# Half a weight tile of large products issued as one block, and the state's products placed later in the chain

## The chip, the core and the metric

The kernel runs on one core of a Trainium2 chip. Each engine of the core works through its own queue in order: TensorE (PE, matrix products), VectorE (DVE), ScalarE (ACT), GpSimd (POOL) and SyncE (SP, which issues DMAs). The metric is the device time of one execution in microseconds; for the kernel before, the median of three runs.

## The reference, cut to what matters

Two layers run over 256 context tokens and 512 latent tokens of width 1024. In each, one input projection feeds three branches; their results are projected, gated, summed and projected again, and an MLP of four times the width follows.

```python
zc, zl = hc @ w_in, hl @ w_in                 # context, latent
def _rwkv_scan(state0, r, decay, k, v, kk, a, reverse):
    def step(S, inp):                         # per head of 64
        s_kk = einsum('bhij,bhj->bhi', S, kk_t)
        S = S * w_t - s_kk * (kk_t * a_t) + v_t * k_t
        return S, einsum('bhij,bhj->bhi', S, r_t)
# branch A: this scan, forward and backward, 16 heads, context before latent
# branch B: depthwise convolution of 31 taps, LayerNorm, silu
# branch C: attention, 8 query heads of 128, 2 key heads
out = sum(gates * (branch @ w_branch)) @ w_out
x = x + rms_norm(out); x = x + rms_norm(square(relu(h @ w1)) @ w2)
```

Layer 1, the last, needs only the latent tokens of the output.

## The kernel before

**Large products.** Every product with a weight matrix is split into three 32-bit products (high by high, low by high, high by low: `hh`/`hl` of the activations, `wh`/`wl` of the weights). A weight column of 128 outputs has eight k-tiles of 128. Half of it (four k-tiles, 128x512) is one transfer: SP issues the DMA into `raw`, ACT makes `wh` from it (L328), POOL or DVE makes `wl` (L330, L332). `fill` (from L397) takes k-tiles from a list of jobs and issues their products on L412. So half a weight tile gives four k-tiles times three terms times the pieces of the tokens: 24 products in layer 0 (768 tokens, two pieces of 384), 12 in most of layer 1 (512 tokens, one piece). The MLP uses `gemm` (L389) instead.

**The rwkv phase.** Branch A walks over eight pairs of heads in each layer. Tokens are cut into 12 chunks of 64. For one pair, in this order: merge of the inverse's blocks (L892, L904), a batch of products (L920, L931), and the chain of 12 steps. A step adds to the state's accumulator `sp` a product that no state enters (L952) and one that the state enters (L956); ACT scales it into the new state `S` (L958); the outputs `yp` take a product of the state (L968) and one without it (L970). Beside the chain run the readout of the pair before (L1005, L1016) and the preparation of the next one: squares of the keys (L717, L700 for their sums by head), the low-rank products (L1032), the scaled keys on DVE (L772 to L784), the bonus (key on L871, product on L877, used on L878). Then come the grams of the next pair (L810, masked on DVE by L814; transposes on L819), and then the solve: DVE inverts triangular blocks by 30 alternating small operations (L861, L862) between transposes (L855, L856 and L863, L864), while PE has the rest of the pair's preparation (L743, L845). The next merge needs L863 and L864. In between DVE evicts what large products deliver: operands of branch A (L658, `in_k`, `in_r`, `in_v`), branch B's input (L463), and it does the 31 taps of the convolution (L473), which are held in program order.

**What sets the order.** The program states a weave: `weave` takes generators, each of which yields an estimate of its time on PE, and calls `fill` in proportion, so that large products are strewn between the small ones. Tile's scheduler then orders each engine's queue by dependence and priority; a product may move past others whose operands are not expected yet. `fill` is also called in attention between the score products (L615) and the transposes of the probabilities (L631) of a block of queries. At the end of each pair `fill` is called for a fixed number of k-tiles that lie over the solve.

Of the kernel before, what the change touches and what calls it, by code (L numbers as in the profile page):

```python
# [8 lines left out]
F32 = mybir.dt.float32  # L9
# [67 lines left out]
class Kern:  # L77
# [314 lines left out]
    def job(s, src, mh, ml, T, done, pre=None):  # L392

        s.halves += [(src, h) for h in range(2)]
        s.jobs += [(k, mh, ml, T, done, pre) for k in range(KT)]

    def fill(s, n=1):  # L397
        nc = s.nc
        for _ in range(min(n, len(s.jobs))):
            k, mh, ml, T, done, pre = s.jobs.pop(0)  # L400
            if k % 4 == 0:
                while s.halves and len(s.ready) < 2:
                    s.ready.append(s.weight_half(*s.halves.pop(0)))
                s.cur = s.ready.pop(0)
            if k == 0:
                s.jps = s.mm()
                s.jctx = (pre(),) if pre else ()
            wh, wl = s.cur
            for w, m, f in ((wh, mh, 0), (wh, ml, 1), (wl, mh, 2)):
                a = m(k)  # L410
                for b, t0, t1 in s.pieces(T):
                    ins = nc.tensor.matmul(s.jps[:, b, :t1 - t0], lhsT=w[:, k % 4, :], rhs=a[:, t0:t1], start=k == 0 and f == 0, stop=k == KT - 1 and f == 2)  # L412
                    if s.pin and f == 0 and b == 0:
                        s.tc.keep_in_program_order(ins)
            if k == KT - 1:
                done(s.jps, *s.jctx)
# [292 lines left out]
    def rw_kk(s, P, p, I):  # L709

        nc = s.nc
        kkc = P['v']('rw_k_k')[:, p:p + 1]
        sq = s.rt("ksq", [128, TOK], alias="a1")
        nc.scalar.activation(out=sq, in_=I['k'], func=AF.Square, scale=kkc)
        sp = s.g([128, 6, 2])
        for t in range(6):
            nc.tensor.matmul(sp[:, t, :], lhsT=sq[:, t * 128:t * 128 + 128], rhs=s.bo[:, 0:128:64], start=True, stop=True)  # L717
# [20 lines left out]
    def rw_transpose(s, src, h, dst):  # L738

        nc = s.nc  # L740
        vp = s.g([128, 6, 64])
        for m in range(6):
            nc.tensor.transpose(out=vp[:, m, :], in_=src[ROWS[h], m * 128:m * 128 + 128], identity=s.ident[ROWS[h], 64 * h:64 * h + 64])  # L743
        nc.scalar.activation(out=dst(0), in_=vp[ROWS[0]], func=AF.Copy)
        nc.scalar.activation(out=dst(1), in_=vp[ROWS[1]], func=AF.Copy)
# [43 lines left out]
    def rw_front(s, I, Q, d, g, lat):  # L789
# [18 lines left out]
        for q in range(4):  # L808
            for h in range(2):
                nc.tensor.matmul(gp[h][:, q, 0:n, :], lhsT=BK[ROWS[h], 4 * g + q].rearrange("p a b -> p (a b)"),  # L810
                                 rhs=KR[ROWS[h], 0:n, 4 * g + q, :], start=True, stop=True)
# [6 lines left out]
        for q in range(4):  # L818
            nc.tensor.transpose(out=bk[:, q].rearrange("p a b -> p (a b)"), in_=BK[:, 4 * g + q].rearrange("p a b -> p (a b)"), identity=s.ident)  # L819
        nc.scalar.activation(out=GB[:, :, c, 0, :], in_=bk.rearrange("p c h j -> p h c j"), func=AF.Copy)  # L820
# [15 lines left out]
    def rw_rest(s, d):  # L836
# [3 lines left out]
        for g, m in ((0, 8), (8, 4)):  # L840
            mv = s.g([128, 8, 64])
            for c in range(g, g + m):
                for h in range(2):
                    w = ROWS[1 - h]
                    nc.tensor.matmul(mv[ROWS[h], c - g, :], lhsT=GL[w, h, c, :], rhs=UV[w, h * 12 + c, :], start=True, stop=True)  # L845
            nc.scalar.activation(out=KM[:, g:g + m, 1, :], in_=mv[:, :m], func=AF.Copy)
            yield 0.16 * m
# [18 lines left out]
    def rw_bonus(s, P, p, I, Q, T):  # L866
# [8 lines left out]
        for b, t0, t1 in s.pieces(T):  # L875
            bp = s.g([128, t1 - t0])
            nc.tensor.matmul(bp, lhsT=s.bo, rhs=ks[:, t0:t1], start=True, stop=True)  # L877
            nc.vector.tensor_tensor(out=bv[:, t0:t1], in0=I['v'][:, t0:t1], in1=bp, op=ALU.mult)  # L878
            yield 0.8
# [3 lines left out]
    def rw_merge(s, Q, d):  # L883
# [6 lines left out]
        for q in range(12):  # L890
            for h in range(2):
                nc.tensor.matmul(xp[two[h], q, :], lhsT=GL[one[h], h, q, c:c + 32], rhs=Dn[one[h], q, :], start=True, stop=True)  # L892
        TT = Q['TT', d] = GL.rearrange("p h c t -> p (h c t)")[:, 0:768].rearrange("p (c t) -> p c t", t=64)
# [8 lines left out]
        for q in range(12):  # L902
            for h in range(2):
                nc.tensor.matmul(tr[one[h], q, :], lhsT=Xn[two[h], q, :], rhs=Dt[two[h], q, :], start=True, stop=True)  # L904
        for h in range(2):
# [3 lines left out]
    def rw_batch(s, Q, d, lat):  # L909
# [6 lines left out]
        for q0 in range(0, 12, 4):  # L916
            wu = s.g([128, 4, 2, 64])
            for q in range(q0, q0 + 4):
                for h in range(2):
                    nc.tensor.matmul(wu[ROWS[h], q - q0], lhsT=TT[ROWS[h], q, :], rhs=KM[ROWS[h], q].rearrange("p a b -> p (a b)"), start=True, stop=True)  # L920
            nc.scalar.activation(out=W[:, q0:q0 + 4], in_=wu[:, :, 0, :], func=AF.Copy)
# [4 lines left out]
        for q0 in range(0, 12, 4):  # L926
            n = 1 if lat and q0 == 0 else 2
            ap = s.g([128, 4, 2, 64])
            for q in range(q0, q0 + 4):
                for h in range(2):  # L930
                    nc.tensor.matmul(ap[ROWS[h], q - q0, 0:n, :], lhsT=W[ROWS[h], q, :], rhs=GB[ROWS[h], h, q, 0:n, :], start=True, stop=True)  # L931
            nc.vector.tensor_tensor(out=KR[:, 0, q0:q0 + 4, :], in0=ap[:, :, 0, :], in1=s.id2.unsqueeze(1).to_broadcast([128, 4, 64]), op=ALU.add)
# [4 lines left out]
    def rw_chain(s, Q, lat, note, free):  # L937
# [5 lines left out]
        for k in range(NCH):  # L943
            q = (k, ORD_B[k])
            need_y = not lat or k >= 4
            seg = 0 if k < 4 else 1
            if k < NCH - 1:
                sp = s.pc.tile([128, 2, 64], F32, tag="c", name="sp")
                Sn = t("S", [128, 2, 64], 2)
                for d in range(2):  # L950
                    for h in range(2):
                        nc.tensor.matmul(sp[ROWS[h], d], lhsT=GB[d][:, h, q[d], 0, :], rhs=UV[d][:, h * 12 + q[d], :], start=d == 0, stop=d == 1 and k == 0)  # L952
                if k:
                    for d in range(2):
                        for h in range(2):
                            nc.tensor.matmul(sp[ROWS[h], d], lhsT=KR[d][ROWS[h], 0, q[d], :], rhs=S[ROWS[h], d], start=False, stop=d == 1)  # L956
                for d in range(2):
                    nc.scalar.activation(out=Sn[:, d], in_=sp[:, d], func=AF.Copy, scale=Q['lam', d][:, q[d]:q[d] + 1])  # L958
            if need_y:
                fresh = seg not in yp  # L960
                if fresh:
                    yp[seg] = s.py.tile([128, 512], F32, tag="y", name="yp")
                for part in ((1, 0) if k else (0,)):
                    for d in range(2):
                        o = (q[d] - 4 * seg) * 64
                        for h in range(2):
# [15 lines left out]
    def rw_readout(s, l, P, p, Q, T, dst):  # L982
# [19 lines left out]
        for b, t0, t1 in s.pieces(T):  # L1002
            R = s.g([128, t1 - t0])
            for c in range(t0, t1, 128):
                nc.tensor.transpose(out=R[:, c - t0:c - t0 + 128], in_=y[:, c:c + 128], identity=s.ident)  # L1005

# [7 lines left out]
        for b, t0, t1 in s.pieces(T):  # L1014
            gp = s.g([128, t1 - t0])
            nc.tensor.matmul(gp, lhsT=Q['g2'], rhs=s.sgd[:, t0:t1], start=True, stop=True)  # L1016
            nc.vector.tensor_tensor(out=y[:, t0:t1], in0=y[:, t0:t1], in1=gp, op=ALU.mult)
# [109 lines left out]
    def rwkv_phase(s, l, P, T):  # L1127
# [3 lines left out]
        with ExitStack() as rc:  # L1131
# [315 lines left out]
```

## Time and profile before

| | |
|---|---|
| median of three runs | 4514.72 us (4509.4 to 4517.8) |
| the profiled execution | 4503.07 us |
| its span, first to last instruction | 4501.3 us |
| mean granted clock of TensorE, as a share of full speed | 0.956 |
| busy PE, DVE, ACT, POOL | 93%, 59%, 42%, 18% |
| large products: L412, L389 (instructions) | 8520, 4608 |

The profile shows one execution. In its rows an instruction is named by its engine, line and operation, then the tile written and the tiles read. A small 32-bit product can leave two records, so that x8 in a row can be four products. Starts are in microseconds from the start of the span; the start of one product to the start of the next says how long it held PE, since the printed duration includes the pipeline. A window gives the busy time of the engines in a stretch. "128*128" behind an operation is the rows and columns of the array that it uses.

### The profile page before, as it was taken

To read this page: it belongs to the slowest core of one execution; us is meant where nothing else is said; L and a number is where in the kernel's file an instruction comes from. 1 tells how busy PE (TensorE), PEld (TensorE's weight loads), DVE (VectorE), ACT (ScalarE), POOL (GpSimd) and SP (SyncE) were. 2 spreads that over 40 slices of the span, in tenths; PEclk is the share of its full clock that TensorE was granted. 3 is DMA by queue.
4 is the path that set the end of the run, shared out by engine and by line. 5 is a ranking of instruction groups with operands and counts; after the bars stand their busy time and mean duration, and the time that the engine had idled before them with its cause. 6 is when DMAs were issued, how large, how long until landed. Compare 5 with 4: busy or idle time off the path is not lost. (4 is left out here: it accounts for less than half of the span.)

```text
span 4501.3 us, 76922 instructions
## 1 busy us (share of the span) xinstructions
PE 4197.0 (93%) x31232; PEld 3411.4 (76%) x31232; DVE 2642.9 (59%) x4762; ACT 1889.5 (42%) x3690; POOL 831.3 (18%) x737
## 2 busy tenths in 40 slices
PE   6999999999998989899999899999999988898998
PEld 4888888888786668689999667877777775475886
DVE  3788788887855443132233568778787845443344
ACT  3455445444534442232223354555555534434333
POOL 0011221212112144300000102122122212262001
PEclk8999999999999999999999889999999979998998
DMA  4211111111224234343322221111111223142332
GB/s 161 62 47 53 57 58 57 51 52 58 73 84 157 71 110 142 126 141 117 107 87 63 69 61 52 50 60 47 56 54 57 75 71 121 57 133 64 96 96 82
DMA packets 438346, 364.05 MB, mean 81 GB/s; under 512 B 19022, under 2 KB 386792, under 8 KB 431848
## 3 DMA queue, kind: packets, MB, share of 16 engines
q1 hardware_dynamic: 417256, 279.43, 20.5%
q10 hardware_dynamic: 20736, 79.70, 4.9%
q8 instruction: 247, 4.05, 0.4%
q14 instruction: 107, 0.88, 0.1%
HBM read 299.29 MB, written 53.48 MB: 78 GB/s over the span
## 5 line engine op out<-in xcount | busy, mean ns | idle before, releaser
L328 ACT ACTIVATE wh<-raw 128x512 fp32r<-128x512 f32 x700 | 441.4, 631 | 1261.5 <-PE mm L389 558.3
L330 POOL TENSOR_TENSOR wl<-raw,wh 128x512 fp32r<-128x512 f32 x388 | 535.5, 1381 | 2062.3 <-ACT wh L328 1699.1
L412 PE MATMUL mm<-hh,wh 128*128 128x384 f32 (+1 forms) x2072 | 668.6, 381 | 49.4 <-ACT wh L328 40.7
L412 PE MATMUL mm<-hl,wh 128*128 128x384 f32 (+1 forms) x2072 | 644.5, 370 | 7.0 <-POOL hl L330 7.0
L412 PE MATMUL mm<-hh,wl 128*128 128x384 f32 (+1 forms) x2072 | 641.4, 369 | 4.9 <-POOL wl L330 4.6
L332 DVE TENSOR_TENSOR wl<-raw,wh 128x512 fp32r<-128x512 f32 x312 | 215.5, 691 | 589.7 <-ACT wh L328 586.4
L412 PEld LDWEIGHTS mm<-hh,wh 128*128 128x128 f32 x2072 | 379.2, 195 | 112.7 <-ACT wh L328 45.6
L473 DVE SCALAR_TENSOR_TENSOR cv<-u,dw,cv 128x783 f32<-128x783 f32 (+1 forms) x480 | 458.3, 955 | 3.1
L412 PEld LDWEIGHTS mm<-hl,wh 128*128 128x128 f32 x2072 | 389.6, 195 | 47.7 <-issue 12.1
L412 PEld LDWEIGHTS mm<-hh,wl 128*128 128x128 f32 x2072 | 388.0, 194 | 47.1 <-POOL wl L330 10.8
L412 PE MATMUL mm<-oh,wh 128*128 128x384 f32 (+1 forms) x768 | 256.7, 389 | 12.1 <-DVE acc L1273 4.1
L412 PE MATMUL mm<-oh,wl 128*128 128x384 f32 (+1 forms) x768 | 245.9, 374 | 22.0 <-POOL wl L330 22.0
L412 PE MATMUL mm<-ol,wh 128*128 128x384 f32 (+1 forms) x768 | 243.5, 370 | 6.6 <-POOL ol L330 5.6
L389 PE MATMUL mm<-hh,wh 128*128 128x384 f32 (+1 forms) x768 | 239.3, 367 | 6.3 <-ACT hh L347 3.6
L389 PE MATMUL mm<-hl,wh 128*128 128x384 f32 (+1 forms) x768 | 238.3, 365 | 5.5 <-POOL hl L330 5.0
L389 PE MATMUL mm<-hh,wl 128*128 128x384 f32 (+1 forms) x768 | 236.0, 362 | 0.0
L389 PE MATMUL mm<-fh,wh 128*128 128x384 f32 (+1 forms) x768 | 230.2, 353 | 0.0
L389 PE MATMUL mm<-fh,wl 128*128 128x384 f32 (+1 forms) x768 | 230.0, 353 | 0.0
L389 PE MATMUL mm<-fl,wh 128*128 128x384 f32 (+1 forms) x768 | 229.8, 353 | 0.0
L862 DVE TENSOR_TENSOR A<-A,Z 128x30 f32<-128x30 f32 (+14 forms) x480 | 198.2, 413 | 15.8
L861 DVE TENSOR_TENSOR Z<-A 128x30 f32<-128x30 f32 (+14 forms) x480 | 190.7, 397 | 16.5
L412 PEld LDWEIGHTS mm<-oh,wh 128*128 128x128 f32 x768 | 143.9, 195 | 55.2 <-ACT wh L328 15.8
(294 smaller groups left out, 7425.6 us busy)
## 6 DMA issues: line engine op xcount, KB each, us to landing
raw<-in_w_in_dram SPq DMA_DIRECT2D x316, 256.0 KB
raw<-in_w_ff_dram SPq DMA_DIRECT2D x256, 256.0 KB
wmod<-in_w_mod_dram ACTq DMA_DIRECT2D x48, 1024.0 KB
raw<-in_w_branch_dram SPq DMA_DIRECT2D x96, 256.0 KB
z<-f ACTq DMA_DIRECT2D x40, 384.0 KB
gt<-z SPq DMA_DIRECT2D x24, 384.0 KB
raw<-in_w_out_dram SPq DMA_DIRECT2D x32, 256.0 KB
z<-f ACTq DMA_DIRECT2D x32, 256.0 KB
```

The source lines that it names most:

```text
L328: nc.scalar.activation(out=hi, in_=src, func=AF.Copy)
L330: nc.gpsimd.tensor_tensor(out=lo, in0=src, in1=hi.bitcast(F32), op=ALU.subtract)
L332: nc.vector.tensor_tensor(out=lo, in0=src, in1=hi.bitcast(F32), op=ALU.subtract)
L389: nc.tensor.matmul(ps[:, b, :t1 - t0], lhsT=w[:, k % 4, :], rhs=a[:, t0:t1], start=k == 0 and f == 0, stop=k == KT - 1 and f == 2)
L412: ins = nc.tensor.matmul(s.jps[:, b, :t1 - t0], lhsT=w[:, k % 4, :], rhs=a[:, t0:t1], start=k == 0 and f == 0, stop=k == KT - 1 and f == 2)
L473: s.tap_pin(nc.vector.scalar_tensor_tensor(out=hold['c'], in0=u[:, k:k + L], scalar=w(k), in1=hold['c'], op0=ALU.mult, op1=ALU.add))
L861: nc.vector.tensor_tensor(out=tm, in0=X[:, k + 1:, k:k + 1].to_broadcast([128, n, k]), in1=X[:, k:k + 1, 0:k].to_broadcast([128, n, k]), o ...
L862: nc.vector.tensor_tensor(out=X[:, k + 1:, 0:k], in0=X[:, k + 1:, 0:k], in1=tm, op=ALU.add)
```

## The change

First, `fill` opens a context around each large product, `keep`: the first product of each half weight tile is issued at its ordinary priority, all others of that half tile under `tc.high_priority()`. Once the first has been placed, the rest come ahead of anything else on PE that is ready. The pin that is removed was never switched on.

Second, a step of the chain is written in another order: L970 of before (now L958), L952 (L964), L956 (L968), the scaling on ACT, L968 (L976). The products that no state enters stand first. The places where `nc` becomes `s.nc` do nothing. Lines after L412 are shifted by 3 to 8; L412 is L417 in the kernel after. Every engine has as many instructions as before.

```diff
+    def keep(s, first):
+
+        return nullcontext() if first else s.tc.high_priority()
...
@@ fill @@
             for w, m, f in ((wh, mh, 0), (wh, ml, 1), (wl, mh, 2)):
                 a = m(k)
                 for b, t0, t1 in s.pieces(T):
-                    ins = nc.tensor.matmul(s.jps[:, b, :t1 - t0], lhsT=w[:, k % 4, :], rhs=a[:, t0:t1], start=k == 0 and f == 0, stop=k == KT - 1 and f == 2)
-                    if s.pin and f == 0 and b == 0:
-                        s.tc.keep_in_program_order(ins)
+                    with s.keep(k % 4 == 0 and f == 0 and b == 0):
+                        nc.tensor.matmul(s.jps[:, b, :t1 - t0], lhsT=w[:, k % 4, :], rhs=a[:, t0:t1], start=k == 0 and f == 0, stop=k == KT - 1 and f == 2)
...
@@ rw_chain @@
+            if need_y:
+                fresh = seg not in yp
+                if fresh:
+                    yp[seg] = s.py.tile([128, 512], F32, tag="y", name="yp")
+                for d in range(2):
+                    o = (q[d] - 4 * seg) * 64
+                    for h in range(2):
+                        s.nc.tensor.matmul(yp[seg][ROWS[h], o:o + 64], lhsT=GB[d][:, h, q[d], 1, :], rhs=UV[d][:, h * 12 + q[d], :], start=fresh and d == 0, stop=False)
             if k < NCH - 1:
...
-            if need_y:
-                fresh = seg not in yp
-                if fresh:
-                    yp[seg] = s.py.tile([128, 512], F32, tag="y", name="yp")
-                for part in ((1, 0) if k else (0,)):
-                    for d in range(2):
-                        o = (q[d] - 4 * seg) * 64
-                        for h in range(2):
-                            if part:
-                                nc.tensor.matmul(yp[seg][ROWS[h], o:o + 64], lhsT=KR[d][ROWS[h], 1, q[d], :], rhs=S[ROWS[h], d], start=fresh, stop=False)
-                            else:
-                                nc.tensor.matmul(yp[seg][ROWS[h], o:o + 64], lhsT=GB[d][:, h, q[d], 1, :], rhs=UV[d][:, h * 12 + q[d], :], start=fresh, stop=d == 1 and k in (3, NCH - 1))
-                        fresh = False
+            if need_y and k:
+                for d in range(2):
+                    o = (q[d] - 4 * seg) * 64
+                    for h in range(2):
+                        s.nc.tensor.matmul(yp[seg][ROWS[h], o:o + 64], lhsT=KR[d][ROWS[h], 1, q[d], :], rhs=S[ROWS[h], d], start=False, stop=d == 1 and k in (3, NCH - 1))
```

On PE, one step of the chain in layer 0's sixth pair (`sp` and `yp` accumulate state and output, `mm` is a large product). Before:

```order
L952 MATMUL sp<-UV_659,GB_658 64x64 x2
L952 MATMUL sp<-UV_665,GB_664 64x64 x2
L956 MATMUL sp<-S,KR_656 64x64 x2
L956 MATMUL sp<-S,KR_662 64x64 x2
L968 MATMUL yp<-S,KR_662 64x64 x2
L970 MATMUL yp<-UV_659,GB_658 64x64 x2
L970 MATMUL yp<-UV_665,GB_664 64x64 x2
L412 MATMUL mm<-hl,wh 128x384
L968 MATMUL yp<-S,KR_656 64x64 x2
L412 MATMUL mm<-hl,wh 128x384
```

After:

```order
L964 MATMUL sp<-UV_659,GB_658 64x64 x2
L964 MATMUL sp<-UV_665,GB_664 64x64 x2
L968 MATMUL sp<-S,KR_656 64x64 x2
L968 MATMUL sp<-S,KR_662 64x64 x2
L976 MATMUL yp<-S,KR_662 64x64 x2
L958 MATMUL yp<-UV_659,GB_658 64x64 x2
L958 MATMUL yp<-UV_665,GB_664 64x64 x2
L976 MATMUL yp<-S,KR_656 64x64 x2
L964 MATMUL sp<-UV_659,GB_658 64x64 x2
L964 MATMUL sp<-UV_665,GB_664 64x64 x2
```

The single large products between the steps are gone, and step follows step; the scheduler still parts the state's two output products (KR_662, KR_656).

On PE in the same place of the next phase, from the last grams (of the pair that follows) into the solve. Before:

```order
L810 MATMUL g<-KR_662,BK_661 128x128 x8
L412 MATMUL mm<-hh,wh 128x384
L412 MATMUL mm<-hl,wh 128x384 x2
L412 MATMUL mm<-hh,wl 128x384 x2
L819 MATMUL g<-cst,BK_661 128x128 x4
L412 MATMUL mm<-hh,wh 128x384 x2
L743 MATMUL g<-cst,in_v 128x64 x12
L412 MATMUL mm<-hl,wh 128x384 x2
L412 MATMUL mm<-hh,wl 128x384 x2
L845 MATMUL g<-UV_659,GL_657 64x64
```

After:

```order
L813 MATMUL g<-KR_656,BK_655 128x128 x8
L822 MATMUL g<-cst,BK_655 128x128 x4
L813 MATMUL g<-KR_662,BK_661 128x128 x8
L822 MATMUL g<-cst,BK_661 128x128 x4
L746 MATMUL g<-cst,in_v 128x64 x12
L848 MATMUL g<-UV_659,GL_657 64x64 x24
L417 MATMUL mm<-hh,wh 128x384 x2
L417 MATMUL mm<-hl,wh 128x384 x2
L417 MATMUL mm<-hh,wl 128x384 x2
```

Grams, transposes and the rest of the preparation now stand in one piece, and a block of 24 follows; before, large products stood between all of them. Five such blocks, 120 products, follow the last gram until the merge, where there were 209.

On DVE at the first masks of the grams of the same pair, behind the bonus. Before:

```order
L803 TENSOR_TENSOR KR_662<-in_kk,KR_662 128x256
L878 TENSOR_TENSOR key<-in_v,g 128x384
L805 TENSOR_TENSOR KR_662<-in_r,KR_662 128x256
L803 TENSOR_TENSOR KR_656<-in_kk,KR_656 128x256
L814 TENSOR_TENSOR GL_657<-g,masks 128x256
L814 TENSOR_TENSOR GB_658<-g,masks 128x4x64
```

After:

```order
L661 SCALAR_TENSOR_TENSOR in_r<-f_9479,H,in_r 128x511
L661 SCALAR_TENSOR_TENSOR in_r<-f_9479,H,in_r 128x255
L661 SCALAR_TENSOR_TENSOR in_r<-f_9479,H,in_r 128x511
L473 TENSOR_SCALAR cv<-u,dw,V 128x783
L476 SCALAR_TENSOR_TENSOR cv<-u,dw,cv 128x783 x3
L817 TENSOR_TENSOR GL_657<-g,masks 128x256
L817 TENSOR_TENSOR GB_658<-g,masks 128x4x64
```

The evictions of the next pair's `in_r` and the first taps of the next convolution column (L473, L476) have come in between the masks.

## Rows read from the trace of the kernel before

**Rows 1.** The page: busy time of each engine over the span, instructions

```profile
PE 4197.0 (93%) x31232; PEld 3411.4 (76%) x31232; DVE 2642.9 (59%) x4762; ACT 1889.5 (42%) x3690; POOL 831.3 (18%) x737
```

**Rows 2.** Busy time in windows (us, five engines; granted clock, DMA share, GB/s)

```profile
966.70:1045.60 78.90, 77.84 (x958) 62.65 (x957) 67.62 (x102) 43.47 (x102) 17.16 (x20) 1.00 0.18 55
981.00:1045.60 64.60, 63.54 (x703) 49.27 (x701) 57.28 (x80) 34.68 (x87) 14.59 (x18) 1.00 0.17 56
...
1067.20:1117.30 50.10, 47.35 (x345) 43.25 (x345) 39.24 (x82) 21.14 (x37) 12.04 (x9) 0.97 0.21 59
3078.90:3150.00 71.10, 66.69 (x805) 49.57 (x806) 57.88 (x98) 43.84 (x101) 14.22 (x18) 0.86 0.13 38
```

**Rows 3.** Waits of PE: us in total, times, longest

```profile
PE mm L412 <- ACT wh L328: 43.8, 15, 7.9
...
PE g L892 <- DVE Z L863: 21.5, 4, 9.0
...
PE g L877 <- DVE key L871: 15.5, 7, 6.4
```

**Rows 4.** Order of time on PE, a stretch of the chain (start us, us)

```profile
1029.29 0.33 PE L968 MATMUL yp<-S,KR 64*64 64x64 f32 x4 [0.35 <-ACT S L958]
...
1029.92 0.45 PE L952 MATMUL sp<-UV,GB 128*64 128x64 f32 x8
1030.30 0.45 PE L956 MATMUL sp<-S,KR 64*64 64x64 f32 x8
1030.58 0.28 PE L968 MATMUL yp<-S,KR 64*64 64x64 f32 x4
...
1031.18 0.44 PE L412 MATMUL mm<-hh,wl 128*128 128x384 f32 x1
1031.55 0.32 PE L968 MATMUL yp<-S,KR 64*64 64x64 f32 x2
```

**Rows 5.** The same view, between grams of layer 0 and of layer 1

```profile
1054.40 0.51 PE L412 MATMUL mm<-hh,wl 128*128 128x384 f32 x2
1054.75 0.60 PE L819 MATMUL g<-cst,BK 128*128 128x128 f32 x4
1055.11 0.60 PE L412 MATMUL mm<-hh,wh 128*128 128x384 f32 x2
1055.63 0.60 PE L810 MATMUL g<-KR,BK 64*128 64x128 f32 x3
...
3169.92 0.40 PE L412 MATMUL mm<-hh,wh 128*128 128x512 f32 x1
3170.16 0.40 PE L412 MATMUL mm<-hl,wh 128*128 128x512 f32 x1
```

**Rows 6.** The same view: PE, DVE (end of the solve), PE again

```profile
980.91 0.49 PE L700 MATMUL g<-cst,rb 128*128 128x128 f32 x3
...
1099.61 2.10 DVE L863 STREAM_TRANSPOSE Z<-A 128x1024 f32<-128x1024 f32 x1
...
1104.91 0.63 PE L412 MATMUL mm<-hh,wh 128*128 128x384 f32 x2 [2.64 <-ACT wh L328]
...
1117.35 1.61 PE L892 MATMUL g<-Z,GL 32*32 32x32 f32 x96
```

**Rows 7.** Windows of the end of layer 1's last pair and of a head alone

```profile
3690.80:3715.00 24.20, 18.77 (x85) 13.95 (x83) 10.04 (x23) 7.36 (x14) 6.42 (x5) 1.00 0.49 159
3838.30:3858.90 20.60, 14.79 (x56) 8.06 (x54) 10.52 (x21) 9.03 (x19) 1.27 (x1) 1.00 0.16 51
```

**Rows 8.** Windows of layer 1's last chain

```profile
3624.50:3648.40 23.90, 23.90 (x290) 18.22 (x289) 14.31 (x25) 14.47 (x40) 2.55 (x2) 1.00 0.37 114
3648.40:3689.30 40.90, 40.90 (x310) 35.08 (x307) 9.68 (x41) 5.06 (x17) 1.28 (x1) 0.50 0.04 14
```

**Rows 9.** Order of time on PE within the second of these windows

```profile
3656.96 0.69 PE L952 MATMUL sp<-UV,GB 128*64 128x64 f32 x8
3657.58 0.69 PE L956 MATMUL sp<-S,KR 64*64 64x64 f32 x6
```

More of the change, by code (lines that the diff above doesn't have):

```diff
@@ L1 @@
-from contextlib import ExitStack
+from contextlib import ExitStack, nullcontext
 import numpy as np
@@ L716, in rw_kk @@
         for t in range(6):
-            nc.tensor.matmul(sp[:, t, :], lhsT=sq[:, t * 128:t * 128 + 128], rhs=s.bo[:, 0:128:64], start=True, stop=True)
+            s.nc.tensor.matmul(sp[:, t, :], lhsT=sq[:, t * 128:t * 128 + 128], rhs=s.bo[:, 0:128:64], start=True, stop=True)
         yield 1.2 + s.sched['sums']
@@ L742, in rw_transpose @@
         for m in range(6):
-            nc.tensor.transpose(out=vp[:, m, :], in_=src[ROWS[h], m * 128:m * 128 + 128], identity=s.ident[ROWS[h], 64 * h:64 * h + 64])
+            s.nc.tensor.transpose(out=vp[:, m, :], in_=src[ROWS[h], m * 128:m * 128 + 128], identity=s.ident[ROWS[h], 64 * h:64 * h + 64])
         nc.scalar.activation(out=dst(0), in_=vp[ROWS[0]], func=AF.Copy)
@@ L818, in rw_front @@
         for q in range(4):
-            nc.tensor.transpose(out=bk[:, q].rearrange("p a b -> p (a b)"), in_=BK[:, 4 * g + q].rearrange("p a b -> p (a b)"), identity=s.ident)
+            s.nc.tensor.transpose(out=bk[:, q].rearrange("p a b -> p (a b)"), in_=BK[:, 4 * g + q].rearrange("p a b -> p (a b)"), identity=s.ident)
         nc.scalar.activation(out=GB[:, :, c, 0, :], in_=bk.rearrange("p c h j -> p h c j"), func=AF.Copy)
@@ L844, in rw_rest @@
                     w = ROWS[1 - h]
-                    nc.tensor.matmul(mv[ROWS[h], c - g, :], lhsT=GL[w, h, c, :], rhs=UV[w, h * 12 + c, :], start=True, stop=True)
+                    s.nc.tensor.matmul(mv[ROWS[h], c - g, :], lhsT=GL[w, h, c, :], rhs=UV[w, h * 12 + c, :], start=True, stop=True)
             nc.scalar.activation(out=KM[:, g:g + m, 1, :], in_=mv[:, :m], func=AF.Copy)
@@ L876, in rw_bonus @@
             bp = s.g([128, t1 - t0])
-            nc.tensor.matmul(bp, lhsT=s.bo, rhs=ks[:, t0:t1], start=True, stop=True)
+            s.nc.tensor.matmul(bp, lhsT=s.bo, rhs=ks[:, t0:t1], start=True, stop=True)
             nc.vector.tensor_tensor(out=bv[:, t0:t1], in0=I['v'][:, t0:t1], in1=bp, op=ALU.mult)
@@ L891, in rw_merge @@
             for h in range(2):
-                nc.tensor.matmul(xp[two[h], q, :], lhsT=GL[one[h], h, q, c:c + 32], rhs=Dn[one[h], q, :], start=True, stop=True)
+                s.nc.tensor.matmul(xp[two[h], q, :], lhsT=GL[one[h], h, q, c:c + 32], rhs=Dn[one[h], q, :], start=True, stop=True)
         TT = Q['TT', d] = GL.rearrange("p h c t -> p (h c t)")[:, 0:768].rearrange("p (c t) -> p c t", t=64)
@@ L903, in rw_merge @@
             for h in range(2):
-                nc.tensor.matmul(tr[one[h], q, :], lhsT=Xn[two[h], q, :], rhs=Dt[two[h], q, :], start=True, stop=True)
+                s.nc.tensor.matmul(tr[one[h], q, :], lhsT=Xn[two[h], q, :], rhs=Dt[two[h], q, :], start=True, stop=True)
         for h in range(2):
@@ L919, in rw_batch @@
                 for h in range(2):
[L920 removed]
+                    s.nc.tensor.matmul(wu[ROWS[h], q - q0], lhsT=TT[ROWS[h], q, :], rhs=KM[ROWS[h], q].rearrange("p a b -> p (a b)"), start=True, stop=True)
             nc.scalar.activation(out=W[:, q0:q0 + 4], in_=wu[:, :, 0, :], func=AF.Copy)
@@ L1004, in rw_readout @@
             for c in range(t0, t1, 128):
-                nc.tensor.transpose(out=R[:, c - t0:c - t0 + 128], in_=y[:, c:c + 128], identity=s.ident)
+                s.nc.tensor.transpose(out=R[:, c - t0:c - t0 + 128], in_=y[:, c:c + 128], identity=s.ident)
             R = R.rearrange("p (m a) -> p m a", a=128)
@@ L1015, in rw_readout @@
             gp = s.g([128, t1 - t0])
-            nc.tensor.matmul(gp, lhsT=Q['g2'], rhs=s.sgd[:, t0:t1], start=True, stop=True)
+            s.nc.tensor.matmul(gp, lhsT=Q['g2'], rhs=s.sgd[:, t0:t1], start=True, stop=True)
             nc.vector.tensor_tensor(out=y[:, t0:t1], in0=y[:, t0:t1], in1=gp, op=ALU.mult)
```

19 lines of the change are left out of this document (9 added, 10 removed).

## Prediction

> **What bounds the kernel now.** I read the page first: TensorE (PE) is busy 93% of the span with VectorE (DVE) at 59% [rows 1]. So PE's order looks like the whole case, and breaks in it like pure loss. The windows of one head pair correct that. I take the pair whose first merge product starts at 966.7 and cut it in three: A, from the merge (L892) to the bonus product (L877); G, from there to the last gram (L810); S, from there to the next merge at 1117.3. In A, PE is busy 77.84 of 78.9 us, but DVE is busy too, 67.62 us, 57.28 of them in the last 64.6 us; in S, DVE is busy 39.24 of 50.1 us with the solve, a serial run of small operations [rows 2]. PE is full there only because large products were spread so that they lie over DVE's work. A second view says where PE waits nevertheless: for the high half weights 43.8 us, in front of the merge for the solve (L863) 21.5, in front of the bonus for its key (L871) 15.5 [rows 3].
>
> **What a break costs.** The chain's rows show one step [rows 4]: the products without the state (L952) from 1029.92, those of the state (L956) from 1030.30, output products 1030.58 to 1031.18, a single large product 1031.18 to 1031.55, then the rest of L968. The large product holds PE for 0.37 us; inside a run one takes 0.17 (two start 0.35 apart, 1054.40 to 1054.75 [rows 5]). So a break looks like 0.20 us. But 8 records of L952 hold PE 0.38 us and 8 of L956 0.28: where one small form follows another, 0.1 us is lost as well, and this stays when the large product between them goes. And from a large product to the transposes of L819, which have its own 128*128 form, nothing is lost (1054.75 is 2 x 0.17 behind 1054.40), while in front of L810 (64*128) it is 0.17 (1055.11 to 1055.63, less 0.35) [rows 5]. I take 0.1 us for a break (ends 0.05 and 0.2).
>
> In the order, L412 stands in 944 unbroken stretches before and 344 after. 600 x 0.1 = 60 us at most (30 to 120). The Trainium skill says the same from the other end ("TensorEngine Tiling (Array Packing)", Key Properties): a change of tiling mode drains TensorE, while another tile of the same mode does not. By that rule the 944 stretches are the wrong thing to count; the order has 1833 changes of form before and 1489 after, and 344 x 0.1 is 34 us; the sum below, in which some 23 us of breaks reach the end (158 outside the pairs, 66 in G), would be 10 us higher. The rows on L819 and L810 agree with the rule.
>
> **Where the breaks go, and what then ends last.** Of the 600, 442 lie in the 14 pairs that are followed by another, and 158 outside them.
>
> Pair at 966.7 (large products before and after, from the order: A 176 and 144, G 35 and 168, S 209 and 120).
> A: PE's own time is 77.84 less 32 x 0.174 and 23 breaks x 0.1, that is 70. DVE sets another floor. Before, 12 us of its work stood ahead of the first operation that needs L700's product (980.91 [rows 6]), evictions and taps; after, 2 us. The operands' evictions (L658) and five of 30 taps have gone behind the bonus. From L700 on there are 54 us of DVE work left (counts from the order, each at its form's duration in the trace). 14.3 + 54 + an idle time of 3 (0 to the 7.3 that it has now in those 64.6 us [rows 2]) is 71.5. So A falls by 7.4, not by the 8.9 that PE alone would give.
> G: 133 x 0.174 less 4 breaks, +22.7. The masks' evictions on DVE are covered there; nothing else is late.
> S: PE's own 47.35 less 89 x 0.174 and 7 breaks is 31. The solve needs 34.5 from the last gram to the end of L863 (1099.61 + 2.10 less 1067.2 [rows 6]), and an eviction or two of the moved L658 stand within it: 36. S falls by 14.1 and PE waits some 5 us in front of the merge, where it waits nothing now (L892 at 1117.35 has no wait in its row, and the 2.64 us in S are one for a high half weight [rows 6]).
> Sum +1.2; the pair holds 12 more large products (2.1 us) that lie elsewhere before, so -0.9 on equal work.
>
> Layer 1, pair at 3078.9 (A 93 and 48, G 24 and 72, S 126 and 132; a large product is 0.24 there, 3169.92 to 3170.16 [rows 5]). A: PE's own falls from 66.69 to 54, DVE's after L700 stays at 43 against 46 us, so 14 + 43 + 3 = 60 against 71.1: -11.1. G +10.9, S +1.0, less 9 x 0.24 of moved work: -1.4. Seven pairs each: 7 x -0.9 and 7 x -1.4 make -16 us, though their 442 breaks are worth 44. The rest is handed to DVE, behind which PE now waits at the bonus and at the merge.
>
> Outside the pairs: 158 breaks, -16 us. Against that stand covers that go. Single large products (L412) are dropped today between the score products of attention. A head without them took 20.6 us with PE busy for 14.79, so 5.8 idle [rows 7]. In the order the heads without cover rise by about 2.8 in layer 1 and 1.5 in layer 0: 4.3 x 5.8 = +25. At the end of a layer's last pair, readout and the opening of attention run serially; in layer 1 that is 24.2 us with PE at 18.77 [rows 7]. In layer 0 it has 399 large products in 44 stretches in front of it today and will have 72 in 3: +10 (5.4 to 24).
>
> **Clock.** The granted clock was 1.00 in A of the pair at 966.7 and 0.86 in that of 3078.9, where fewer large products stand. After 3648.4 it was 0.50 for 40.9 us in a stretch with few of them, behind 23.9 us at 1.00 [rows 8]. There 8 records of L952 take 0.62 us from start to start, where 0.38 is the rule [rows 4, 9]. The order makes the chain nearly free of large products: the longest stretch without one averages 202 products per pair, at most 66 before. 202 at 0.35 us for four are 18 us; at half clock 29, so +11 for a pair where it falls. Nothing shows whether it will; I take one pair in five, 2 us each, 14 x 2 = +28 (0 to 98, below).
>
> **Second edit.** In the chain the state-free output products (L970) move ahead of the state's. The chain itself did not wait: S is ready before the next S products, and only PE products behind a large product wait for it (0.35 us at 1029.29 [rows 4]). Worth nothing to -0.35 in each of the 15 steps with one lone large product: 0 to -5, taken as 0.
>
> **Sum.** -16 - 16 + 25 + 10 + 28 = +31 on the profiled execution's 4503.07, so 4534. That execution lies 11.7 under the median of 4514.72; on the median's footing 4546, rounded to **4545**.
>
> **Rivals.**
> Cover stays (faster): DVE and solve are not later than PE, and attention loses nothing, since weights ready early let large products slip in. For it: A's DVE share is already 86% today with only small waits [rows 2, 3]. Against: 120 large products are 20.9 us, and with the other products 31, less than the solve's 34.5. Price: the full 60 us, at the upper end 120: 4395 to 4485, centre 4455.
> Cancelling: clock costs nothing and the waits just eat the breaks: within 9 us of 4515.
> Half clock in the chain (slower still): every pair's stretch without large products falls to 1.2 GHz. A hides 2 us of it in layer 0 and 6 in layer 1 (PE's own against DVE's floor), so 7 x 9 + 7 x 5 = 98 instead of 28. Decided by whether the small products alone keep the clock up. Against: 3624.5 to 3648.4 shows 23.9 us of mostly small products at 1.00 [rows 8]. 4545 + 70 = 4615.
> The change not doing what it says: blocks still broken, because a wanted operand is late. The order shows 297 of 344 stretches of 12 or 24, so under 3%; left in the second case.
>
> **How the numbers follow.** Forecast as summed, 4525 to 4590: 0.40. Cover stays, 4395 to 4500: 0.33. Cancelling, 4506 to 4524: 0.14. Half clock, 4600 to 4660: 0.13. The range leaves out the lower third of the faster case and the upper half of the last: 4445 to 4625. A measurement tells apart about 0.2%, 9 us: faster 0.33, same 0.14, slower 0.53.
>
> **What would show it.** Right: in windows A, G, S of the pairs, G some 23 us longer in layer 0, S near 36 with a wait for L863's successor in front of the merge in most pairs; waits at the bonus of 1 to 3 us; DVE's share of A unchanged; heads without large products near 20 us. Wrong in the step on cover: no wait at the merge, S at PE's own 31. Wrong on the clock: a mean granted clock above today's 0.956, or under 0.90. Wrong on the price: a mean step of the chain not 0.2 to 0.5 us shorter than today's.

## The result, and the profile after

The changed kernel takes 4723.51 us (4721.58 to 4725.54), the kernel before 4515.36: 1.0463 of it, interval 1.0445 to 1.0481. 4545 was forecast; the time lies above the range. The profiled execution has a span of 4720.6 us, 219 more than before.

The page's first line answers to [rows 1], and the line with the clock gives the whole span's mean:

```profile
PE 4252.7 (90%) x31232; PEld 3536.0 (75%) x31232; DVE 2609.4 (55%) x4762; ACT 1892.2 (40%) x3690; POOL 813.1 (17%) x737
```

```profile
die 0 (median of its cores): 4720.6 us, clock 0.915
```

PE is busy 56 us longer though it issues the same products in 600 fewer stretches, and idle 164 us longer. The clock was 0.956 before: time at half clock (1.2 of 2.4 GHz) has gone from some 396 us to some 802 (1 - 0.915 is half of the share spent there).

The segments, from the starts of the merge's first product; on the right the difference less the large products that moved from one segment to another (0.174 us each with 384 columns, 0.24 with 512):

| segment | before | after | difference | on equal work |
|---|---|---|---|---|
| up to the first merge | 232.0 | 268.9 | +36.9 | +3.5 |
| seven pairs of layer 0 | 1019.6 | 1122.8 | +103.2 | +78 |
| last pair, attention, merge, MLP, opening of layer 1 | 1429.6 | 1428.2 | -1.4 | +30 |
| seven pairs of layer 1 | 932.9 | 1007.8 | +74.9 | +86 |
| last pair to the end | 887.2 | 892.9 | +5.7 | +23 |

PE's waits answer to [rows 3] (total, times, longest):

```profile
PE g L895 <- DVE Z L866: 73.8, 13, 8.4
PE g L880 <- DVE key L874: 56.4, 9, 9.8
...
PE mm L417 <- ACT wh L328: 13.9, 7, 4.8
```

The high half weights are hardly waited for any more (13.9 us, 43.8 before); the merge is (73.8, 21.5 before), and the bonus (56.4, 15.5). In the seven pairs of layer 0 PE does not wait at the bonus at all; in those of layer 1 it does so in each, for 4.5 to 6.5 us.

Windows of the changed kernel (columns as in [rows 2]): A of the fourth pair in three parts and whole, then G and S of the sixth pair, then a G of layer 1. The last line is A of the fourth pair in the kernel before:

```profile
739.70:770.00 30.30, 29.21 (x406) 27.29 (x406) 16.73 (x30) 18.77 (x40) 5.75 (x4) 0.89 0.17 50
770.00:790.00 20.00, 16.53 (x235) 11.84 (x232) 18.67 (x36) 6.86 (x22) 0.21 (x2) 0.97 0.06 24
790.00:821.90 31.90, 28.26 (x243) 21.00 (x242) 23.63 (x27) 15.90 (x40) 2.90 (x10) 0.54 0.05 17
739.70:821.90 82.20, 74.00 (x877) 60.12 (x877) 59.02 (x91) 41.52 (x100) 8.86 (x16) 0.77 0.10 31
1145.00:1189.40 44.40, 43.43 (x289) 39.83 (x287) 21.72 (x43) 15.88 (x28) 10.17 (x8) 1.00 0.19 57
1189.40:1224.40 35.00, 31.23 (x259) 28.96 (x259) 32.78 (x77) 14.27 (x26) 5.40 (x4) 0.90 0.26 76
3467.80:3504.00 36.20, 36.20 (x188) 31.16 (x190) 14.87 (x35) 11.99 (x23) 4.05 (x4) 0.76 0.12 37
...
677.60:754.30 76.70, 75.64 (x945) 60.67 (x944) 68.35 (x101) 43.45 (x101) 16.23 (x19) 1.00 0.17 53
```

G of the sixth pair is 44.4 us and S 35.0, both near what was reckoned (44.3 and 36). A is not: in the fourth pair it takes 82.2 us with only 96 large products, where it took 76.7 with 164 before. PE is busy for 74 of the 82.2 us and DVE for 59, so neither's work alone fills it. From 790 on the clock is 0.54. In layer 1's G it is 0.76.

The order of time on PE just there shows how it comes to that:

```profile
786.46 0.91 PE L1037 MATMUL g<-low,lw 64*128 64x384 f32 x2 [0.79 <-DVE y L1022]
788.04 0.92 PE L1037 MATMUL g<-low,lw 64*128 64x384 f32 x4 [0.67 <-ACT sg L756]
789.62 2.12 PE L1037 MATMUL g<-low,lw 64*128 64x384 f32 x4 [0.67 <-ACT A L756]
791.94 1.64 PE L1037 MATMUL g<-low,lw 64*128 64x384 f32 x2 [0.20 <-ACT A L756]
...
798.20 0.69 PE L964 MATMUL sp<-UV,GB 128*64 128x64 f32 x8
798.83 0.69 PE L968 MATMUL sp<-S,KR 64*64 64x64 f32 x8
```

Low-rank products (L1037) wait four times running, once for VectorE and three times for ScalarE, with no large product to put between. Before, large products and steps of the chain stood among the low-rank products of this pair, and PE did not wait there:

```profile
724.70 0.91 PE L1032 MATMUL g<-low,lw 64*128 64x384 f32 x2
725.54 0.62 PE L412 MATMUL mm<-hh,wl 128*128 128x384 f32 x2
```

Now PE waits 2.3 us in 6, and then the same eight records of L964 hold it for 0.63 us (798.20 to 798.83) where [rows 4] have 0.38. The next large product comes at 815.98. The whole stretch without one is 51.4 us long, from 764.6; in the kernel before the longest of a pair was 7.6 us or less.

### The profile page after: what moved, and what is told of

It is laid out like the page before. It is cut to its first block, busy times and chain, and to the rows that moved or that the text cites. A ratio compares the mean times of both kernels' runs of the same rounds, so it can differ in the third digit from the quotient of the medians.

```text
span 4720.6 us, 76967 instructions
## 1 busy us (share of the span) xinstructions
PE 4252.7 (90%) x31232; PEld 3536.0 (75%) x31232; DVE 2609.4 (55%) x4762; ACT 1892.2 (40%) x3690; POOL 813.1 (17%) x737
## 5 line engine op out<-in xcount | busy, mean ns | idle before, releaser
L330 POOL TENSOR_TENSOR wl<-raw,wh 128x512 fp32r<-128x512 f32 x388 | 521.5, 1345 | 2039.1 <-ACT wh L328 1669.1
L417 PE MATMUL mm<-hh,wh 128*128 128x384 f32 (+1 forms) x2072 | 656.4, 381 | 31.0 <-ACT cv L458 16.9
L417 PE MATMUL mm<-hl,wh 128*128 128x384 f32 (+1 forms) x2072 | 619.3, 364 | 6.7 <-POOL hl L330 6.7
L417 PE MATMUL mm<-hh,wl 128*128 128x384 f32 (+1 forms) x2072 | 615.8, 362 | 0.3 <-POOL wl L330 0.3
L476 DVE SCALAR_TENSOR_TENSOR cv<-u,dw,cv 128x783 f32<-128x783 f32 (+1 forms) x480 | 460.7, 960 | 4.1
L417 PEld LDWEIGHTS mm<-hh,wh 128*128 128x128 f32 x2072 | 389.0, 199 | 80.0 <-ACT cv L458 17.8
L417 PEld LDWEIGHTS mm<-hl,wh 128*128 128x128 f32 x2072 | 400.6, 199 | 28.0 <-POOL hl L330 9.7
L417 PEld LDWEIGHTS mm<-hh,wl 128*128 128x128 f32 x2072 | 397.2, 197 | 25.7 <-DVE wl L332 2.1
L417 PE MATMUL mm<-oh,wl 128*128 128x384 f32 (+1 forms) x768 | 240.7, 368 | 25.5 <-POOL wl L330 25.3
L417 PE MATMUL mm<-oh,wh 128*128 128x384 f32 (+1 forms) x768 | 251.1, 382 | 12.8 <-ACT wh L328 7.3
L417 PE MATMUL mm<-ol,wh 128*128 128x384 f32 (+1 forms) x768 | 241.1, 369 | 7.1 <-POOL ol L330 6.8
L389 PE MATMUL mm<-hh,wh 128*128 128x384 f32 (+1 forms) x768 | 239.0, 366 | 6.4 <-ACT hh L347 3.6
L389 PE MATMUL mm<-hl,wh 128*128 128x384 f32 (+1 forms) x768 | 238.1, 364 | 5.5 <-POOL hl L330 5.0
L389 PE MATMUL mm<-hh,wl 128*128 128x384 f32 (+1 forms) x768 | 235.6, 362 | 0.0
L864 DVE TENSOR_TENSOR Z<-A 128x30 f32<-128x30 f32 (+14 forms) x480 | 205.0, 427 | 15.6
L817 DVE TENSOR_TENSOR GL<-g,masks 128x256 f32<-128x256 f32 x192 | 80.6, 421 | 239.6 <-PE g L813 239.1
L813 PEld LDWEIGHTS g<-KR,BK 64*128 64x128 f32 x1536 | 172.7, 216 | 45.4 <-issue 34.0
```

What stands on the lines that cost most here:

```text
L330: nc.gpsimd.tensor_tensor(out=lo, in0=src, in1=hi.bitcast(F32), op=ALU.subtract)
L389: nc.tensor.matmul(ps[:, b, :t1 - t0], lhsT=w[:, k % 4, :], rhs=a[:, t0:t1], start=k == 0 and f == 0, stop=k == KT - 1 and f == 2)
L476: s.tap_pin(nc.vector.scalar_tensor_tensor(out=hold['c'], in0=u[:, k:k + L], scalar=w(k), in1=hold['c'], op0=ALU.mult, op1=ALU.add))
L813: s.nc.tensor.matmul(gp[h][:, q, 0:n, :], lhsT=BK[ROWS[h], 4 * g + q].rearrange("p a b -> p (a b)"), rhs=KR[ROWS[h], 0:n, 4 * g + q, :], s ...
L817: nc.vector.tensor_tensor(out=G, in0=gp[h][:, :, x, :], in1=s.mask(d, h, x).unsqueeze(1).to_broadcast([128, 4, 64]), op=ALU.mult)
L864: nc.vector.tensor_tensor(out=tm, in0=X[:, k + 1:, k:k + 1].to_broadcast([128, n, k]), in1=X[:, k:k + 1, 0:k].to_broadcast([128, n, k]), o ...
```

## The experiments

All times are medians; before is 4512 to 4516 in each group. In the expectations T1 stands for lost cover, T2, T4 and C for the clock in one form or another, T3 for the chain's order.

**Which edit.** e1 has the blocks alone, e2 the chain's new order alone.

```diff
-        return nullcontext() if first else s.tc.high_priority()
+        return nullcontext()
```

(e2; e1 is the kernel before with `fill` of the changed one.)

> The blocks of half a weight tile alone; the chain's step in the old order. Theory T1 (blocks of 24 products take the large products away from beside VectorE's work, so TensorE and VectorE wait for each other in turn): the order has 341 stretches of large products and the same split of the pairs as the changed kernel, so 4690 to 4740 us. Rival T3 (the new order in the chain costs a good part): 4520 to 4620 us.

> The chain's new order alone; large products placed as before (932 stretches). T1: within 0.3% of the kernel before, 4500 to 4530 us. T3: 4600 us or more.

e1: 4727.07, 1.0469 (1.0453 to 1.0485). e2: 4498.68, 0.9963 (0.9948 to 0.9978). The blocks make all of the loss; the chain's order alone gains 17 us, which neither the prediction nor the expectations had.

**How large a block.** The first product of every k-tile (e5), or of every second (e6), is left at ordinary priority.

```diff
-                    with s.keep(k % 4 == 0 and f == 0 and b == 0):
+                    with s.keep(f == 0 and b == 0):
```

> Blocks of one k-tile (6 large products in layer 0, 3 in layer 1) instead of four; 694 stretches, 250 fewer than before, and the products lie in the pairs nearly as before (sixth pair 186, 42, 192 against 176, 35, 209 before and 144, 168, 120 in the changed kernel). T1: waits near those of before, so 4480 to 4530 us. Rival T2 (the half clock behind stretches of small products is the whole loss, cover or not): stretches without a large product are at most 73 products, so the clock stays as before and the time too, 4480 to 4530; T1 and T2 part in the waits at merge and bonus of e6.

> Blocks of two k-tiles (12 and 6 products), 518 stretches. T1: the loss grows with the block, since the split of the pairs moves half the way (sixth pair 168, 96, 144): 4540 to 4620 us, waits at merge and bonus between 37 and 130 us in sum. T2: no stretch without large products is over 84 products, so the clock is that of before and the time 4500 to 4530 us.

e5: 4476.20, 0.9912 (0.9897 to 0.9928), faster than both kernels and than either theory expected. e6: 4547.65, 1.0071 (1.0054 to 1.0088), with 99 us of waits at merge and bonus:

```profile
die 0 (median of its cores): 4545.3 us, clock 0.941
```

```profile
PE g L895 <- DVE Z L866: 74.8, 14, 9.5
...
PE g L880 <- DVE key L874: 24.5, 8, 10.1
```

These are T1's figures, and the statement that stretches of at most 84 products leave the clock alone falls. But the merge is waited for as long here as in the changed kernel (74.8 and 73.8 us), which is 176 us slower: that wait by itself does not make the loss.

**Where.** A flag turns the blocks on only within `rwkv_phase` (e3) or only outside (e4). In e7 and e8 the size of a block is set by where it is filled: `k % s.blk`, with `s.blk` 1 in the weave of chain and preparation and 4 elsewhere (e7), or the reverse (e8).

```diff
+                s.blk = 1
                 s.weave(F['first'] if more else F['last'], *gs)
+                s.blk = 4
```

> Blocks of half a weight tile only in the rwkv phase, large products elsewhere placed as before. T1 (the loss is made in the pairs, where cover goes): most of the 209 us remain, 4660 to 4710 us. Rival (a quarter or more of the loss comes from attention, merge and the layers' openings, as the segments' sums suggest): 4640 to 4670 us.

> The opposite: blocks only outside the rwkv phase. 851 stretches against 932 with the chain's order alone. T1: attention loses single products between its score products, 4505 to 4540 us against 4499 with the chain's order alone. Rival (breaks count, cover doesn't): 81 breaks at 0.1 to 0.2 us gain, 4480 to 4492 us.

> Blocks of one k-tile for what is filled in the weave of chain and preparation, blocks of four elsewhere; 417 stretches, the longest stretch without large products still 106 to 272 products in most pairs, solve cover as in the changed kernel. T4 (the clock falls in stretches of small products and these waits and half clock make the loss): 4580 to 4670 us with a clock of 0.92 to 0.94. T1 alone (cover at merge and bonus): half the way, 4560 to 4620, clock 0.94 or more.

> The opposite: blocks of four k-tiles for what is filled in the weave, blocks of one elsewhere; 610 stretches, and because of the order in which the blocks come due no stretch without large products is over 90 products, with 132 to 174 large products over the solve in layer 0. T4 and T1: waits as with blocks of one k-tile (4476), so 4460 to 4500 us, clock 0.95. Rival (size of the block itself hurts): 4540 us or more.

e3: 4716.93 (more than the 4640 to 4710 that the two theories expected); e4: 4508.89, 10 more than e2. So blocks cost some 5 to 15 us outside the rwkv phase: 7 and 10 by the medians, 5 and 15 by the ratios to the kernel before of each group. With blocks in that phase alone e3 has +36 and +17 on equal work in the third and the last segment, where the changed kernel has +30 and +23: what the segments show there comes with the blocks of the rwkv phase, which takes in each layer's last pair and uses up large products earlier. e7: 4669.71, 1.0346 (1.0331 to 1.0362). e8: 4516.40, 1.0001 (0.9989 to 1.0013), above the 4460 to 4500 expected. Blocks of 24 in the weave cost 40 us against e5, and nothing against the kernel before, where no stretch without large products is over 90. Clock and waits (merge, bonus) of e7 and then e8:

```profile
die 0 (median of its cores): 4668.2 us, clock 0.927
```

```profile
PE g L895 <- DVE Z L866: 101.4, 16, 9.2
PE g L880 <- DVE key L874: 52.1, 9, 9.8
```

```profile
die 0 (median of its cores): 4512.2 us, clock 0.949
```

```profile
PE g L895 <- DVE Z L866: 64.3, 12, 10.2
...
PE g L880 <- DVE key L874: 9.9, 3, 7.1
```

The size of a block is the smaller part of it. What parts e7 from e8 is the stretch that the blocks leave empty (up to 266 products in e7): clock and the bonus's wait go with it.

**The clock.** Added large products stand in front of each step's products into `sp`, written beside them in the same bank and read by nobody: two (e9), six (e14).

```diff
-                sp = s.pc.tile([128, 2, 64], F32, tag="c", name="sp")
+                spf = s.pc.tile([128, 512], F32, tag="c", name="sp")
+                sp = spf[:, 0:128].rearrange("p (a b) -> p a b", b=64)
+                for w in range(6):
+                    s.nc.tensor.matmul(spf[:, 128:512], lhsT=s.hh[:, 0, TOK - 128:], rhs=s.hh[:, w, TOK - 384:], start=True, stop=True)
```

> The changed kernel with two added large products (128x384, their result read by nobody) in front of each step's products into sp: 352 more products, 61 us at 0.174 plus 176 breaks at 0.1 to 0.2, so +79 to +96 us of pure work; the order keeps the blocks, the covers and the waits' places. Theory C (the half clock in the chain is itself a cause): half clock and the time behind it fall by more than the added work, 4600 to 4720 us, clock 0.94 or more. Rival B (the clock only shows that PE waits): 4780 to 4830 us.

> The changed kernel with six added large products in front of each step's products into sp, their result read by nobody: 1056 products, 184 us at 0.174 plus 176 breaks at 0.1 to 0.2, +200 to +219 us of work. Theory C (too few large products bring the chain to half clock, which costs about as much as the clock's excess of 110 us): the clock rises to 0.94 or more and the time is 4740 to 4840 us. Rival B (the clock stays low or its rise is worth nothing): 4870 us or more.

e9: 4766.22, between both, with the clock where it was (0.918): undecided. e14: 4728.27 (4719.43 to 4737.67), 5 us over the changed kernel with 1056 products more, 184 us of work and the breaks, and below what either theory expected. Its clock, and A of the fourth pair, cut as above:

```profile
die 0 (median of its cores): 4717.3 us, clock 0.955
```

```profile
751.20:781.50 30.30, 29.77 (x420) 27.72 (x422) 17.44 (x34) 19.53 (x41) 5.75 (x4) 0.90 0.20 62
781.50:801.50 20.00, 19.75 (x201) 15.39 (x197) 19.18 (x31) 5.38 (x16) 1.99 (x1) 1.00 0.11 38
801.50:831.90 30.40, 30.00 (x330) 22.88 (x328) 24.83 (x32) 16.53 (x39) 6.78 (x10) 1.00 0.06 18
751.20:831.90 80.70, 79.52 (x945) 65.99 (x945) 61.45 (x97) 41.44 (x96) 14.51 (x15) 0.96 0.13 40
```

The clock is that of the kernel before. A takes 80.7 us where it took 82.2, though it holds 120 large products instead of 96 and 60 added ones, and PE is busy 5.5 us longer in it; the last part is at 1.00. The bonus is waited for 14.4 us instead of 56.4, the merge as before:

```profile
PE g L895 <- DVE Z L866: 72.4, 12, 8.4
...
PE g L880 <- DVE key L874: 14.4, 3, 9.8
```

Busy time of the chain's four products and the low-rank ones, before, after and in e14 (count, busy, mean ns, idle before):

```profile
L1032 PE MATMUL g<-low,lw 64*128 64x384 f32 x256 | 94.5, 533 | 3.8 <-ACT A L753 2.8 <-ACT sg L753 0.6 <-ACT A L768 0.4
L952 PE MATMUL sp<-UV,GB 128*64 128x64 f32 x1408 | 87.9, 238 | 0.0
L968 PE MATMUL yp<-S,KR 64*64 64x64 f32 x1216 | 86.5, 230 | 0.4 <-ACT S L958 0.4
L956 PE MATMUL sp<-S,KR 64*64 64x64 f32 x1280 | 79.7, 235 | 0.0
L970 PE MATMUL yp<-UV,GB 128*64 128x64 f32 x1280 | 74.5, 238 | 0.0
```

```profile
L964 PE MATMUL sp<-UV,GB 128*64 128x64 f32 x1408 | 105.7, 253 | 2.4 <-ACT S L971 2.4
L1037 PE MATMUL g<-low,lw 64*128 64x384 f32 x256 | 101.4, 576 | 13.0 <-ACT A L756 6.3 <-ACT sg L756 2.7 <-ACT A L771 2.1
...
L976 PE MATMUL yp<-S,KR 64*64 64x64 f32 x1216 | 99.9, 258 | 6.4 <-ACT S L971 4.6 <-DVE st L279 0.5 <-DVE rq L279 0.5
...
L958 PE MATMUL yp<-UV,GB 128*64 128x64 f32 x1280 | 92.9, 260 | 0.0
L968 PE MATMUL sp<-S,KR 64*64 64x64 f32 x1280 | 85.9, 251 | 1.3 <-DVE KR L935 1.3
```

```profile
L1040 PE MATMUL g<-low,lw 64*128 64x384 f32 x256 | 92.4, 531 | 3.3 <-ACT A L756 2.2 <-ACT sg L756 0.7
L967 PE MATMUL sp<-UV,GB 128*64 128x64 f32 x1408 | 91.0, 237 | 0.1
L979 PE MATMUL yp<-S,KR 64*64 64x64 f32 x1216 | 88.7, 228 | 2.0 <-ACT S L974 0.8 <-DVE rq L279 0.5
L958 PE MATMUL yp<-UV,GB 128*64 128x64 f32 x1280 | 82.3, 236 | 0.0
L971 PE MATMUL sp<-S,KR 64*64 64x64 f32 x1280 | 77.7, 233 | 0.0
```

They sum to 423, 486 and 432 us: 63 us more for the same products, and 54 of them back in e14.

All start-to-start intervals on PE, sorted by the granted clock and each priced at the median of the same two neighbours at full clock, give an account of the span, but for some 20 us at its ends: products slowed by half clock 117 us before, 228 after, 111 in e14; waits (all other time beyond the price) 809, 922 and 834; the rest 3553, 3550 and 3752. So of the 219 us about 110 are slowed products and 113 waits, and 202 us of added work took the place of 117 and 88 of these. It is an estimate: told apart more finely or more coarsely, the same neighbours give 98 to 115 us of slowed products and 111 to 141 of waits. Some 46 of the slowed 110 us lie in A of layer 0 and some 51 in G of layer 1, behind the wait at the bonus; A of layer 1 has only 4.

This much is shown: where large products are put back, both go. Whether the clock falls with the waits or with the missing large products as such, e14 does not part. Other rows have the one without the other. In e6 blocks of six stand between the steps of the chain in two pairs of layer 1 until just before the bonus; one bonus is waited for 3.64 us, the other 0.34. The two bonus products, and the windows of G from each on:

```profile
3178.17 2.08 PE L880 MATMUL g<-key,cst 128*128 128x512 f32 x2 [3.64 <-DVE key L874]
...
3456.20 1.13 PE L880 MATMUL g<-key,cst 128*128 128x512 f32 x2 [0.34 <-DVE key L874]
```

```profile
3178.20:3206.20 28.00, 28.00 (x154) 24.52 (x154) 13.56 (x33) 7.83 (x16) 1.27 (x1) 0.71 0.09 30
...
3456.20:3480.50 24.30, 23.79 (x166) 20.53 (x166) 14.27 (x33) 8.49 (x18) 4.05 (x3) 1.00 0.20 64
```

So the clock fell in a wait that had large products right in front of it (at 3177.6). In the last chain of the kernel before it fell to 0.50 without any wait: PE is busy in all of both windows of [rows 8], with 19 large products in the 23.9 us at 1.00 and 10 in the 40.9 us at 0.50. Which of the two it is in A of layer 0, where both come together, stays open.

**VectorE's share.** In e10 (changed) and e11 (before) the solve's loop ends at step 15 of 30; in e12 and e13 ten of 30 taps are left out.

```diff
-        for k in range(1, 31):
+        for k in range(1, 16):
...
-            s.cops = [tap0] + [lambda k=k: tap(k) for k in range(1, CONV_W)] + [store]
+            s.cops = [tap0] + [lambda k=k: tap(k) for k in range(1, CONV_W - 10)] + [store]
```

> The changed kernel with the solve's steps 16 to 30 left out (half of the small operations on VectorE between two transposes, about 12 us less in each of 16 solves). T1 (the solve has lost its cover): the 93 us of waits in front of the merge go, and some half clock behind them: 4590 to 4650 us. Theory C alone (all is made in the chain): 4690 to 4720 us.

> The same left out of the kernel before (solve's steps 16 to 30). There PE waits 21.5 us for the solve and 43.8 for high half weights that stand behind it on ScalarE: 4450 to 4500 us by T1 and by theory C.

> The changed kernel with ten of the 30 scaled taps of the convolution left out: 10.8 us less on VectorE in a pair of layer 0, 7.4 in layer 1. If VectorE's backlog sets the stretch up to the bonus, as the prediction put it: 4600 to 4670 us, waits at the bonus under 15 us. Theory C (TensorE's own small products at half clock and their chain over ScalarE set it): 4690 to 4720 us.

> The kernel before with ten of the 30 scaled taps left out (the control of the same cut in the changed kernel, which gave 4600). If VectorE's backlog is what the change made costly: 4470 to 4500 us, a gain well under the 123 us there. If VectorE's length counts in both alike: 4390 to 4430 us.

The halved solve gains 121 us in the changed kernel (4602.48) and 105 before (4410.74; 4450 to 4500 was expected). So before, too, the solve stood on the path. With hardly a wait left at the merge in either, the changed kernel is still 192 us slower, so the solve's lost cover explains some 16 us of the loss, not 93. The ten taps gain 124 (4599.92) and only 41 before (4472.76): VectorE's length costs three times as much in the changed kernel. The bonus's waits, e12 and then e13 (56.4 and 15.5 with all taps; under 15 was expected of e12):

```profile
PE g L880 <- DVE key L874: 16.2, 3, 9.9
```

```profile
PE g L877 <- DVE key L871: 11.3, 2, 6.4
```

The order shifts somewhat with the work left out, so these are differences of two orders each.

**What is left of a gain.** e15 is e5 with the chain's old order; e16 is e5 with `solve` raised by 4 k-tiles in both layers.

> Blocks of one k-tile without the chain's new order. If the two edits add up: 4476 + 17 = 4485 to 4500 us. If the new order only pays with blocks: 4510 us or more; if it is the blocks that pay: 4480 or less.

> Blocks of one k-tile and the chain's new order, with four more k-tiles called for over each solve (layer 0: 36, layer 1: 44). The 40 us that PE waits in front of the merge with blocks of one k-tile would fall: 4455 to 4475 us. If they only move from the weave's cover: 4475 to 4500 us.

e15: 4476.20, 0.9923 (0.9907 to 0.9939), the same as e5: with blocks of a k-tile the chain's order brings nothing more. e16: 4487.43, 11 us more than e5: PE waits 51.4 us at the merge where e5 has 40.4, so what was called for over the solve did not shorten that wait.

## Why the prediction was wrong

The sign was right and so was the reason that it rests on, that breaks are not what ends last; the size was off by 180 us. The step that failed is A: its time was taken as the work of the busier engine with 3 us of idle time, and 2 us on top for the clock.

- **Break.** 0.1 us was taken, with ends 0.05 and 0.2. e15 has 244 stretches fewer than before and is 38 us faster: 0.16 each if all of the gain is put to them, though its waits differ too. That is in the range, and as said, nothing of it is left in the pairs.
- **G and S.** G of the sixth pair was to be 44.3 and is 44.4; the solve was to end 34.5 after the last gram and does so after 34.8; S 36, measured 35.0, with waits of 2.6 to 5.2 us at the merge of layer 0's pairs in place of 5. In layer 1 no such wait was reckoned, since 132 large products were thought enough: it is 7 to 8 us in most pairs there.
- **A**, the step that failed. For the sixth pair the reckoning had 14.3 us up to the first product of L700, 54 of VectorE's work behind it and 3 of idle time, together 71.5 (they add up to 71.3). Measured are 16.4, 55.5 and 7.7, that is 79.6; the four pairs before it take 80 to 84.5. In the fourth the three are 17.0, 55.0 and 10.2. So the work was right and the idle time was not: behind that product VectorE is idle for 10.2 us and PE for 7.1, both at once for only 1.6. Preparation goes from PE over ScalarE to VectorE and back, several times, and without large products between, the engines wait for each other in turn. The reckoning added up each engine's work and took the larger; the path runs over both. In layer 1, 60 was reckoned and 62.7 to 74.9 measured, with 4.5 to 6.5 us of waits at the bonus where 1 to 3 were named. (The window for it ended at 3150.0, 2 us ahead of the bonus at 3152.05, so A took 73.2 before, not 71.1.) Over the 14 pairs A takes 8 us more than before, where the two pairs' figures times seven make 130 less; G is 34 us above its forecast and S 7 below.
- **Clock**, the term that was mis-sized. 28 us were taken, one pair in five, ends 0 and 98; slowed products make about 110. The longest stretch of a pair without a large product has 199 products in the mean, as reckoned (202), but lasts 40 us and not 18: it was priced at the chain's 0.35 us for four, and it holds longer products, waits and the half clock itself. The rival that prices it (half clock in the chain, 0.13) is what happened in four of layer 0's seven pairs, where A ran at 0.76 to 0.80, but not in layer 1: there G is slow, behind the bonus's wait, for which no rival had a price. So this rival, too, was priced at half. The row that spoke against it (3624.5 to 3648.4 at 1.00 [rows 8]) had 19 large products in it; the stretches now have none and are 16 to 55 us long. The sign named for an error here, a mean clock under 0.90, did not show at 0.915.
- **Outside the pairs** +19 was reckoned (25 + 10 - 16); the third and the last segment have +53 on equal work. By e3 and e4 little of it comes from blocks outside the rwkv phase. The rest, a last pair and attention with fewer large products, was under-priced: some 15 us of it are products slowed by the clock, which the heads' price of 5.8 us of idle time leaves out. How the remainder is shared between last pair and attention stays open.
- **Chain's order**: 0 was taken, -5 at the most. Alone it brings -17 (interval -10 to -23), with blocks of a k-tile nothing. Why stays open.

By the Trainium skill's page "TensorEngine Tiling (Array Packing)" (Key Properties), a change of tiling mode drains TensorE, so changes of mode would count, 344 fewer, and not stretches. No run here parts that from 0.1 us for a break, since the losses are larger than what either gives.

## What to carry to other kernels

In this kernel strewn large products did two jobs beside their own: they filled the waits of a chain that runs over three engines, and where they were put back TensorE's mean clock rose from 0.915 to 0.955. Before they are gathered into blocks, look for the longest stretch that will be left without any, price it with its waits and at half clock, and choose the block so that none appears: here blocks of a k-tile (six products in layer 0) gained 0.9%, blocks of 24 cost 4.6%. The work of the busiest engine is only a lower bound where the work passes between engines several times; the idle time must be reckoned along the path.

## What the runs showed of the hardware

202 us of added work cost 5 us, because some 117 us of slowed products and 88 us of waits went in exchange (e14). At granted clocks of 0.54 against 1.00 eight records of the chain took 0.63 us instead of 0.38. Two added products per step left the mean clock at 0.918, six brought it to 0.955. The clock fell in a single wait of 3.64 us with large products right in front of it (e6), and it fell in the last chain of the kernel before with PE busy throughout [rows 8].
